# Attention scores on the two halves of the TensorE array: three 64-row matmuls per component in place of two 128-row ones

## The chip, the cores and the metric

The kernel runs on one core of a Trainium2 chip. The metric is the device time of one execution in microseconds, and the figure quoted is the median of several runs. Inputs, outputs and intermediate tiles are float32; large matmuls read float32 data through TensorE's fp32r form.

## What is computed

One layer of a hybrid encoder over 2048 positions of width 1024: a normalised input is projected, four heads of differential attention and four heads of a gated linear recurrence (HGRN2) work side by side on the projection, an output projection and a residual follow, and then a gated feed-forward block with a short convolution. The part that matters here is the differential attention. Each head has two components with 64 features, `q` and `k` are normalised, and the mask lets a query see all keys up to the end of its own chunk of 64:

```python
s = jnp.einsum('bqhcd,bkhcd->bhcqk', qb, k).astype(jnp.float32) * scale
p = jax.nn.softmax(jnp.where(mask, s, -jnp.inf), axis=-1)
a = p[:, :, 0] - lam * p[:, :, 1]
return jnp.einsum('bhqk,bkhe->bqhe', a.astype(v.dtype), v)
```

## The kernel before

The work has four stages: the mixer (projections, attention, recurrence), the output projection, the up projection with the convolution, and the down projection. The change is in the mixer.

The mixer runs four times over the sequence, once for each head `s` (lines 256 to 514). A pass goes over eight blocks of 256 positions, two query tiles of 128 each, so there are 16 query tiles in a pass and 64 in all. For a block, `get_h` fetches the normalised and transposed input as a high and a low part, `proj_a`, `proj_b` and `proj_c` project it with `mm3` (lines 252 to 254, three fp32r matmuls for each eighth of the depth), `trans_qk` transposes q and k, `attn` makes scores and exponentials, `attn_o` combines the two components, transposes the result and multiplies by v, and `hgrn` and `hgrn_o` do the recurrence.

float32 accuracy out of fp32r matmuls comes from splitting an operand into a high part and the remainder. For the scores, `proj_a` writes each normalised 64-feature vector twice, side by side (`qn` with a factor 2, one GpSimd instruction at line 290). `trans_qk` then has four transposes (line 300), and after them 128 rows hold the same 64 features twice. ScalarE writes the high parts (lines 302 and 304). VectorE writes the low part of q (line 305), and in k it overwrites the lower 64 rows with the low part (line 307). A 128-row matmul with the doubled high part of q against this k gives q_high times (k_high + k_low) in one go, and a second one with the low part of q adds the rest:

```python
PE.matmul(sc[:, c0:c0 + cwd], lhsT=qT[:, 0, c, :], rhs=kt[:, c, 0:cwd], start=True, stop=False)
PE.matmul(sc[:, c0:c0 + cwd], lhsT=qT[:, 1, c, :], rhs=kt[:, c, 0:cwd], start=False, stop=True)
```

`attn` handles a query tile in segments of up to 1024 keys (`SEG`), one component after the other. A step of segment and component fills the PSUM tile `sc` (two banks, and only one buffer, `SCB` = 1), sets the masked corner (line 360), takes the maximum on VectorE (line 362), and takes the exponential with its sum on ScalarE (line 373, which is an ACTIVATE and an ACTIVATION_READ_ACCUMULATOR). With a second segment the running maximum (line 365), a correction factor (line 367) and the corrected sum (line 377) are kept. `attn_o` rescales the first segment (line 396), adds the weighted second component (line 400), transposes (line 406), copies (line 408) and multiplies with v (line 411).

The strings `ORDER`, `O0` and `OF` (lines 874 to 876) set in which order the steps of the blocks are written down. The framework's planner then orders the instructions of each engine from data dependencies, free buffers and this order, so that in the trace the matmuls of the score steps stand among those of projections, recurrence and value products. The program on the chip is this fixed order; an engine waits at an instruction whose inputs are late, with all behind it.

Of the kernel before, what the change touches and what calls it, by code (L numbers as in the profile page):

```python
# [18 lines left out]
P = 128  # L19
# [15 lines left out]
NU = S // BLK  # L35
# [27 lines left out]
def hymba_kernel(ctx, tc, x, ln1_w, w_in, q_norm_w, k_norm_w, lam_q1, lam_k1, lam_q2, lam_k2,  # L63
# [25 lines left out]
    ident = cst.tile([P, P], F32, name="ident")  # L89
# [24 lines left out]
    neglam = few.tile([P, 1], F32, name="neglam")  # L114
# [70 lines left out]
    with ExitStack() as ms:  # L185
# [70 lines left out]
        for s in range(4):  # L256
# [16 lines left out]
            def proj_a(b, j):  # L273
                hT = HT_[b]
                kb = b // 2
                if b % 2 == 0 and j == 0:
                    kst[kb] = kv.tile([P, 2, 512], F32R, name="kst", tag="kst")
# [8 lines left out]
                ACT.activation(out=qn[:, :, 0, :], in_=qr, func=AF.Square)  # L286
                ss = sm.small([P, 4], F32, name="ssq", tag="ssq", bufs=2)
                DVE.tensor_reduce(out=ss, in_=qn[:, :, 0, :], axis=AX.X, op=ALU.add)
                r = rstd(sm, ss, 4, 64, "rq")
                POOL.tensor_tensor(  # L290
                    out=qn, in0=qr.rearrange("p g (o e) -> p g o e", o=1).broadcast_to([P, 4, 2, 64]),
                    in1=r.rearrange("p (g o e) -> p g o e", o=1, e=1).broadcast_to([P, 4, 2, 64]), op=ALU.mult)
                QN[b, j] = qn

            def trans_qk(b, j):
                qn = QN.pop((b, j))
                ko = ((2 * b + j) % 4) * P
                tp = pa.tile([P, 4, P], F32, name="tpq", tag="pj", bufs=PJB)
                for g in range(4):
                    PE.transpose(tp[:, g, :], qn[:, g].rearrange("p a e -> p (a e)"), ident)  # L300
                qT = wk.tile([P, 2, 2, P], F32R, name="qT", tag="qT", bufs=QTB)
                ACT.activation(out=qT[:, 0], in_=tp[:, 0:2], func=AF.Copy, scale=qkw[:, 0:1])
                kd = kst[b // 2][:, :, ko:ko + P]
                ACT.activation(out=kd, in_=tp[:, 2:4], func=AF.Copy, scale=qkw[:, 1:2])
                DVE.scalar_tensor_tensor(out=qT[:, 1], in0=tp[:, 0:2], scalar=qkw[:, 0:1],
                                         in1=qT[:, 0].bitcast(F32), op0=ALU.mult, op1=ALU.subtract)
                DVE.scalar_tensor_tensor(out=kd[64:], in0=tp[64:, 2:4], scalar=qkw[64:, 1:2],
                                         in1=kd[64:].bitcast(F32), op0=ALU.mult, op1=ALU.subtract)
                QS[b, j] = qT

            def proj_b(b, j):
# [27 lines left out]
            def attn(b, j):  # L339
                i = 2 * b + j  # L340
                n = (i + 1) * P
                segs = [(k0, min(n, k0 + SEG)) for k0 in range(0, n, SEG)]
                two = len(segs) > 1
                qT = QS.pop((b, j))
                pt = {}
                nms = {}
                ls = {}
                ws = [None, None]
                for si, (k0, k1) in enumerate(segs):
                    for c in range(2):  # L350
                        w = k1 - k0
                        sc = ps.tile([P, SEG], F32, name="sc", tag="sc", bufs=SCB)
                        last = si == len(segs) - 1
                        for c0 in range(0, w, 512):
                            cwd = min(512, w - c0)
                            kt = kst[(k0 + c0) // 512]
                            PE.matmul(sc[:, c0:c0 + cwd], lhsT=qT[:, 0, c, :], rhs=kt[:, c, 0:cwd], start=True, stop=False)  # L357
                            PE.matmul(sc[:, c0:c0 + cwd], lhsT=qT[:, 1, c, :], rhs=kt[:, c, 0:cwd], start=False, stop=True)  # L358
                        if last:
                            DVE.memset(sc[0:64, w - 64:w], -3.0e38)  # L360
                        nm = sm.small([P, 1], F32, name="nm", tag="nm", bufs=8)
                        DVE.tensor_reduce(out=nm, in_=sc[:, 0:w], axis=AX.X, op=ALU.max, negate=True)  # L362
                        if si > 0:
                            nm2 = sm.small([P, 1], F32, name="nm2", tag="nm", bufs=8)
                            DVE.tensor_tensor(out=nm2, in0=nm, in1=nms[c], op=ALU.min)
                            wv = sm.small([P, 1], F32, name="wv", tag="wv", bufs=8)
                            ACT.activation(out=wv, in_=nms[c], func=AF.Exp, scale=-1.0, bias=nm2)
                            ws[c] = wv
                            nm = nm2
                        nms[c] = nm  # L370
                        p = pb.tile([P, SEG], F32, name="p", tag="p")
                        l = sm.small([P, 1], F32, name="l", tag="l", bufs=16)
                        ACT.activation(out=p[:, 0:w], in_=sc[:, 0:w], func=AF.Exp, bias=nm, accum_out=l)  # L373
                        pt[si, c] = p
                        if si > 0:
                            l2 = sm.small([P, 1], F32, name="l2", tag="l", bufs=16)
                            DVE.scalar_tensor_tensor(out=l2, in0=ls[c], scalar=ws[c], in1=l, op0=ALU.mult, op1=ALU.add)
                            l = l2
                        ls[c] = l
                AT[b, j] = (pt, ls, ws, segs, two, i)  # L380

            def attn_o(b, j):
                pt, ls, ws, segs, two, i = AT.pop((b, j))
                r1 = sm.small([P, 2], F32, name="r1", tag="r12")
                DVE.reciprocal(out=r1[:, 0:1], in_=ls[0])
                DVE.reciprocal(out=r1[:, 1:2], in_=ls[1])
                cc = sm.small([P, 2], F32, name="cc", tag="cc")
                DVE.scalar_tensor_tensor(out=cc[:, 0:1], in0=ls[0], scalar=r1[:, 1:2], in1=neglam, op0=ALU.mult, op1=ALU.mult)
                av = ps.tile([P, 512], F32, name="av", tag=AVT, bufs=AVB)
                if two:  # L390
                    DVE.tensor_tensor(out=cc[:, 1:2], in0=cc[:, 0:1], in1=ws[1], op=ALU.mult)
                for si, (k0, k1) in enumerate(segs):
                    w = k1 - k0
                    a = pt[si, 0]
                    if two and si == 0:
                        DVE.tensor_scalar(out=a[:, 0:w], in0=a[:, 0:w], scalar1=ws[0], scalar2=None, op0=ALU.mult)
                        c_ = cc[:, 1:2]
                    else:
                        c_ = cc[:, 0:1]
                    DVE.scalar_tensor_tensor(out=a[:, 0:w], in0=pt[si, 1][:, 0:w], scalar=c_, in1=a[:, 0:w],  # L400
                                             op0=ALU.mult, op1=ALU.add)
                    for c0 in range(0, w, 512):
                        nk = min(512, w - c0) // P
                        tp = ps.tile([P, 4, P], F32, name="tpa", tag="m", bufs=MB)
                        for kk in range(nk):
                            PE.transpose(tp[:, kk, :], a[:, c0 + kk * P:c0 + (kk + 1) * P], ident)
                        aT = wk.tile([P, 4, P], F32, name="aT", tag="aT", bufs=ATB)
                        ACT.copy(aT[:, 0:nk], tp[:, 0:nk])
                        for kk in range(nk):
                            kt = (k0 + c0) // P + kk  # L410
                            PE.matmul(av[:, 0:P], lhsT=aT[:, kk, :], rhs=vst[kt // 4][:, kt % 4, :],  # L411
                                      start=kt == 0, stop=kt == i)
# [466 lines left out]
SCB, PJB, MB = 1, 2, 2  # L879
# [33 lines left out]
```

## Time and profile before

| | |
|---|---|
| median of 3 runs | 2813.1 us (2809.25 to 2815.34) |
| the profiled execution, its own time | 2810.73 us |
| its span | 2809.0 us |
| busy share of the span | PE 96%, PE weight load 84%, DVE 70%, ACT 43%, POOL 39% |
| mean granted TensorE clock | 0.988 of full speed |
| end of the mixer's score steps | about 1253 us after the start of the span |

A matmul's recorded duration covers its way through the array, and the next one begins before it ends. The engine's price of a matmul is therefore the distance from its start to the next start, which a timeline shows, and not the mean duration in a group. PEld is the loading of the stationary operand, which goes beside the matmuls. A row of a group gives line, engine, operation, output and inputs, shape and count, then the busy time in us, the mean duration in ns, and the idle time of the engine just before with what ended it.

### The profile page before, as it was taken

Reading aid. Unit: us, or ns where it says so; the run is one execution under the profiler, and the core shown is the slowest. Engines: PE = TensorE matmul, PEld = TensorE weight load, DVE = VectorE, ACT = ScalarE, POOL = GpSimd, SP = SyncE. Lnnn points to the kernel's source line nnn. Section 1 sums busy time; section 2 is a strip of 40 time slices with the busy share of each in tenths; the row PEclk is TensorE's granted clock in tenths of the full one; section 3 lists DMA queues with packets and bytes.
Section 4 is the critical chain, followed back from the end, with each engine's and each line's share of the span. In section 5 each row is a group of like instructions: output and inputs, shape, how many; then the busy total and the mean of one; then the engine's idle time right before and its main releaser. Section 6 shows DMA issues by size and latency. Waiting matters only on the chain.

```text
span 2809.0 us, 42869 instructions
## 1 busy us (share of the span) xinstructions
PE 2687.4 (96%) x15298; PEld 2349.5 (84%) x15298; DVE 1967.7 (70%) x4049; ACT 1198.3 (43%) x2814; POOL 1090.6 (39%) x1137
## 2 busy tenths in 40 slices
PE   7999999999999999989999999999999998997988
PEld 7998999999999999978877888887888876786866
DVE  4677855676568656673338666678777779889898
ACT  4455533454345434453434444354433444333331
POOL 3232222222222222221244434434334347777775
PEclk9999999999999999999999999999999999999999
DMA  5222312131112221125753222234222224655665
GB/s 185 98 83 97 119 68 72 64 121 68 68 69 88 74 74 64 38 90 191 250 179 123 90 80 78 90 128 135 83 75 90 83 90 158 220 207 187 217 229 190
DMA packets 245557, 331.33 MB, mean 118 GB/s; under 512 B 16367, under 2 KB 203103, under 8 KB 241247
## 3 DMA queue, kind: packets, MB, share of 16 engines
q1 hardware_dynamic: 245342, 328.59, 34.8%
q8 instruction: 121, 1.98, 0.3%
q14 instruction: 94, 0.76, 0.1%
HBM read 223.67 MB, written 104.86 MB: 117 GB/s over the span
## 4 chain that ended last, share of the span: by engine, by line
PE 70%; DVE 15%; POOL 5%; ACT 4%; issue 4%; DMA 2%; SPq 0%; DVEq 0%; POOLq 0%; ACTq 0%
PE q L680 9%; PE q L679 9%; PE q L678 9%; PE pj L252 4%; PE pj L254 4%; PE pj L253 4%; DVE SG L612 4%; PE av L411 4%; PE lt L436 3%; DVE TW L612 2%; PE sc L357 2%; PE pjc L253 2%; PE pjc L252 2%; PE pjc L254 2%; PE pjo L594 2%
## 5 line engine op out<-in xcount | busy, mean ns | idle before, releaser
L800 PE MATMUL pd<-TW,SG 128*128 128x512 f32 x616 | 247.4, 402 | 36.8 <-DVE acc L806 15.1
L679 PE MATMUL q<-xT,WS 128*128 128x512 f32 x704 | 274.4, 390 | 2.4 <-DVE xT L612 2.4
L678 PE MATMUL q<-xT,WS 128*128 128x512 f32 x704 | 274.2, 390 | 0.5 <-ACT xT L611 0.5
L680 PE MATMUL q<-xT,WS 128*128 128x512 f32 x704 | 274.1, 389 | 0.3 <-DVE WS L612 0.3
L801 PE MATMUL pd<-TW,SG 128*128 128x512 f32 x616 | 246.2, 400 | 10.5 <-DVE TW L612 10.4
L802 PE MATMUL pd<-TW,SG 128*128 128x512 f32 x616 | 244.4, 398 | 1.8 <-DVE SG L612 1.8
L611 ACT CAST WS<-st 128x512 fp32r<-128x512 f32 x176 | 108.5, 618 | 244.1 <-PE q L680 230.2
L679 PE MATMUL q<-xB,WS 128*128 128x512 f32 x528 | 206.5, 391 | 2.3 <-DVE xB L612 2.3
L680 PE MATMUL q<-xB,WS 128*128 128x512 f32 x528 | 206.5, 392 | 0.9 <-DVE WS L612 0.9
L678 PE MATMUL q<-xB,WS 128*128 128x512 f32 x528 | 206.2, 391 | 1.1 <-ACT xB L611 1.0
L373 ACT ACTIVATE p<-sc,nm 128x1024 f32<-128x1024 f32 (+4 forms) x192 | 165.6, 862 | 96.9 <-DVE nm L362 96.0
L612 POOL TENSOR_TENSOR WS<-st,WS 128x512 fp32r<-128x512 f32 x44 | 87.2, 1982 | 279.4 <-ACT WS L611 272.5
L362 DVE TENSOR_REDUCE nm<-sc 128x1 f32<-128x1024 f32 (+4 forms) x192 | 174.2, 908 | 18.5 <-PE sc L358 16.2
L252 PE MATMUL pj<-WA,hT 128*128 128x384 f32 x512 | 176.6, 345 | 2.6 <-DVE hT L239 2.6
L800 PEld LDWEIGHTS pd<-TW,SG 128*128 128x128 f32 x616 | 118.8, 193 | 69.6 <-DVE acc L806 13.2
L254 PE MATMUL pj<-WA,hT 128*128 128x384 f32 x512 | 175.6, 343 | 0.0
L253 PE MATMUL pj<-WA,hT 128*128 128x384 f32 x512 | 175.5, 343 | 0.0
L679 PEld LDWEIGHTS q<-xT,WS 128*128 128x128 f32 x704 | 132.3, 188 | 30.6 <-DVE xT L612 3.1
L678 PEld LDWEIGHTS q<-xT,WS 128*128 128x128 f32 x704 | 132.4, 188 | 28.3 <-ACT xT L611 0.9
L680 PEld LDWEIGHTS q<-xT,WS 128*128 128x128 f32 x704 | 132.3, 188 | 28.2 <-DVE WS L612 0.7
L611 ACT CAST WS<-rawu 128x512 fp32r<-128x512 f32 x132 | 82.1, 623 | 161.3 <-PE q L680 160.8
L801 PEld LDWEIGHTS pd<-TW,SG 128*128 128x128 f32 x616 | 119.1, 193 | 37.8 <-DVE TW L612 13.3
(415 smaller groups left out, 8014.5 us busy)
## 6 DMA issues: line engine op xcount, KB each, us to landing
hT<-hTd SPq DMA_DIRECT2D x24, 2048.0 KB, 8.9
rawu<-in_w_up_dram SPq DMA_DIRECT2D x176, 256.0 KB, 3.0
od<-acc SPq DMA_DIRECT2D x48, 512.0 KB, 3.4
acc<-od SPq DMA_DIRECT2D x46, 512.0 KB, 4.4
gd<-c SPq DMA_DIRECT2D x176, 128.0 KB, 1.9
G<-gd SPq DMA_DIRECT2D x24, 768.0 KB, 4.7
xt<-in_x_dram SPq DMA_DIRECT2D x32, 512.0 KB, 4.1
hTd<-hT SPq DMA_DIRECT2D x8, 2048.0 KB, 7.9
```

What stands on the lines that cost most here:

```text
L252: PE.matmul(dst, lhsT=lh, rhs=rh, start=dt == 0, stop=False)
L253: PE.matmul(dst, lhsT=lh, rhs=rl, start=False, stop=False)
L254: PE.matmul(dst, lhsT=ll, rhs=rh, start=False, stop=dt == ND - 1)
L362: DVE.tensor_reduce(out=nm, in_=sc[:, 0:w], axis=AX.X, op=ALU.max, negate=True)
L611: ACT.copy(dst[:, 0], src)
L612: eng.tensor_tensor(out=dst[:, 1], in0=src, in1=dst[:, 0].bitcast(F32), op=ALU.subtract)
L678: PE.matmul(dst, lhsT=w[:, 0, cs], rhs=b_[:, 0, dt], start=dt == 0, stop=False)
L679: PE.matmul(dst, lhsT=w[:, 0, cs], rhs=b_[:, 1, dt], start=False, stop=False)
L680: PE.matmul(dst, lhsT=w[:, 1, cs], rhs=b_[:, 0, dt], start=False, stop=dt == 3)
L800: PE.matmul(pd, lhsT=Sx[n][:, 0, k], rhs=w[:, 0], start=k == 0, stop=False)
L801: PE.matmul(pd, lhsT=Sx[n][:, 0, k], rhs=w[:, 1], start=False, stop=False)
L802: PE.matmul(pd, lhsT=Sx[n][:, 1, k], rhs=w[:, 0], start=False, stop=k == len(qs) - 1)
```

## The change

Each 64-feature vector of q and k is written once; a transpose handles two components at a time, so `trans_qk` has two of them, and rows 0 to 63 hold the first component and rows 64 to 127 the second. q and k each get a high and a low part in full. The scores of a component are three matmuls with 64 rows (high by high, high by low, low by high), and the six of both components alternate between the upper and the lower rows. A segment has 512 keys, and the two banks of `sc` hold both components of it. One reduction takes both maxima; the exponentials are two instructions. A running maximum is kept for each segment, and all correction factors of a query tile are made at its end.

```diff
-TOP, FEW, SMALL, SMALL2 = 480, 192, 320, 192
+TOP, FEW, SMALL, SMALL2 = 480, 192, 256, 192
-SEG = 1024
+SEG = 512
...
-                qn = pp.tile([P, 4, 2, 64], F32, name="qn", tag="qn")
+                qn = pp.tile([P, 4, 64], F32, name="qn", tag="qn")
...
+                POOL.tensor_tensor(out=qn, in0=qr, in1=r.rearrange("p (g e) -> p g e", e=1).broadcast_to([P, 4, 64]),
+                                   op=ALU.mult)
...
-                tp = pa.tile([P, 4, P], F32, name="tpq", tag="pj", bufs=PJB)
-                for g in range(4):
-                    PE.transpose(tp[:, g, :], qn[:, g].rearrange("p a e -> p (a e)"), ident)
-                qT = wk.tile([P, 2, 2, P], F32R, name="qT", tag="qT", bufs=QTB)
+                tp = pa.tile([P, 2, P], F32, name="tpq", tag="pj", bufs=PJB)
+                for g in range(2):
+                    PE.transpose(tp[:, g, :], qn[:, 2 * g:2 * g + 2].rearrange("p a e -> p (a e)"), ident)
+                qT = wk.tile([P, 2, P], F32R, name="qT", tag="qT", bufs=QTB)
                 kd = kst[b // 2][:, :, ko:ko + P]
...
+                for g, d in enumerate((qT, kd)):
+                    ACT.activation(out=d[:, 0], in_=tp[:, g], func=AF.Copy, scale=qkw[:, g:g + 1])
+                    DVE.scalar_tensor_tensor(out=d[:, 1], in0=tp[:, g], scalar=qkw[:, g:g + 1],
+                                             in1=d[:, 0].bitcast(F32), op0=ALU.mult, op1=ALU.subtract)
...
+                for si in range(ns):
+                    w = min(SEG, n - si * SEG)
+                    kt = kst[si]
+                    sc = ps.tile([P, 2, SEG], F32, name="sc", tag="sc", bufs=SCB)
+                    for k, (x, y) in enumerate(((0, 0), (0, 1), (1, 0))):
+                        for c in range(2):
+                            cs = slice(64 * c, 64 * c + 64)
+                            PE.matmul(sc[:, c, 0:w], lhsT=qT[cs, x, :], rhs=kt[cs, y, 0:w], start=k == 0, stop=k == 2)
+                    if si == ns - 1:
+                        DVE.memset(sc[0:64, :, w - 64:w], -3.0e38)
+                    DVE.tensor_reduce(out=nm[:, si], in_=sc[:, :, 0:w], axis=AX.X, op=ALU.max, negate=True)
+                    if si:
+                        DVE.tensor_tensor(out=nm[:, si], in0=nm[:, si], in1=nm[:, si - 1], op=ALU.min)
+                    p = pb.tile([P, 2, SEG], F32, name="p", tag="p")
+                    for c in range(2):
+                        ACT.activation(out=p[:, c, 0:w], in_=sc[:, c, 0:w], func=AF.Exp, bias=nm[:, si, c:c + 1],
+                                       accum_out=l[:, c, si:si + 1])
+                    pt.append((p, w))
+                if ns > 1:
+                    fac = sm.small([P, 2, 4], F32, name="fac", tag="fac", bufs=4)
+                    for c in range(2):
+                        ACT.activation(out=fac[:, c, 0:ns], in_=nm[:, 0:ns, c], func=AF.Exp, scale=-1.0,
+                                       bias=nm[:, ns - 1, c:c + 1])
+                    DVE.tensor_tensor(out=l[:, :, 0:ns], in0=l[:, :, 0:ns], in1=fac[:, :, 0:ns], op=ALU.mult)
+                    ls = sm.small([P, 2], F32, name="ls", tag="ls", bufs=4)
+                    DVE.tensor_reduce(out=ls, in_=l[:, :, 0:ns], axis=AX.X, op=ALU.add)
...
+                for si, (p, w) in enumerate(pt):
+                    a = p[:, 0, 0:w]
+                    c_ = cc[:, 0:1]
+                    if si < ns - 1:
+                        DVE.tensor_scalar(out=a, in0=a, scalar1=fac[:, 0, si:si + 1], scalar2=None, op0=ALU.mult)
+                        c_ = cc[:, 1 + si:2 + si]
+                    DVE.scalar_tensor_tensor(out=a, in0=p[:, 1, 0:w], scalar=c_, in1=a, op0=ALU.mult, op1=ALU.add)
```

The transposes, copies and value products of `attn_o` stay one set for each 512 keys, as they were.

## Rows read from the trace of the kernel before

**Rows 1.** Busy time of each engine in stretches of the span. The first four rows are the mixer from its first score step on, the fifth is the mixer with its start, and the sixth is all that follows. Columns: stretch, its length, then busy us and instructions (x) of PE, PEld, DVE, ACT and POOL, the granted TensorE clock, the DMA share, GB/s.
```profile
45.00:350.00 305.00, 294.72 (x2141) 278.63 (x2139) 217.48 (x695) 162.52 (x452) 81.49 (x145) 0.98 0.29 102
350.00:650.00 300.00, 294.42 (x2167) 278.12 (x2166) 199.93 (x651) 136.40 (x398) 73.08 (x130) 1.00 0.22 76
650.00:950.00 300.00, 293.83 (x2160) 277.08 (x2159) 199.24 (x653) 135.36 (x396) 73.89 (x131) 1.00 0.23 78
950.00:1258.00 308.00, 291.65 (x2103) 272.96 (x2102) 202.69 (x649) 134.03 (x383) 77.50 (x124) 0.98 0.19 66
0.00:1258.00 1258.00, 1203.27 (x8735) 1133.48 (x8736) 840.48 (x2688) 589.75 (x1671) 322.87 (x572) 0.99 0.25 86
1258.00:2809.00 1551.00, 1484.11 (x6565) 1215.99 (x6563) 1127.22 (x1362) 608.53 (x1143) 767.72 (x565) 0.99 0.44 144
```

**Rows 2.** The page's chain of work that ended last, its shares of the span by engine.
```profile
PE 70%; DVE 15%; POOL 5%; ACT 4%; issue 4%; DMA 2%; SPq 0%; DVEq 0%; POOLq 0%; ACTq 0%
```

**Rows 3.** Waits of the mixer (0 to 1258 us): who waited for whom, us in total, times, the longest in us.
```profile
PEld sc L357 <- ACT p L373: 16.7, 39, 1.7
PEld lt L436 <- DVE kS L445: 13.2, 23, 3.6
PE sc L357 <- ACT p L373: 6.1, 6, 1.5
```

**Rows 4.** Groups of PE in the mixer, shapes kept apart: the score matmuls by their number of keys, and the transposes of q and k.
```profile
L357 PE MATMUL sc<-kst,qT 128*128 128x512 f32 x224 | 97.3, 435 | 6.7 <-ACT p L373 5.7
L300 PE MATMUL tpq<-ident,qn 128*128 128x128 f32 x256 | 39.4, 272 | 0.0
L357 PE MATMUL sc<-kst,qT 128*128 128x384 f32 x32 | 12.5, 389 | 0.5 <-ACT p L373 0.3
L357 PE MATMUL sc<-kst,qT 128*128 128x256 f32 x32 | 10.1, 316 | 0.0
L357 PE MATMUL sc<-kst,qT 128*128 128x128 f32 x32 | 8.6, 270 | 0.2
```

**Rows 5.** Timeline of PE around 567 us, matmuls with 256 columns one behind the other. Columns here and in the other timelines: start in us, duration in us, engine, line, operation, output and inputs, shape, count.
```profile
566.54 0.28 PE L252 MATMUL pjc<-hT,WC 128*128 128x256 f32 x1
...
567.26 0.28 PE L252 MATMUL pjc<-hT,WC 128*128 128x256 f32 x1
```

**Rows 6.** Timeline of PE around 577 us: matmuls with 384 columns, then the four of a score step with 1024 keys, then 384 columns again.
```profile
575.74 0.33 PE L254 MATMUL pj<-WA,hT 128*128 128x384 f32 x1
...
576.61 0.40 PE L357 MATMUL sc<-kst,qT 128*128 128x512 f32 x1
576.84 0.40 PE L358 MATMUL sc<-kst,qT 128*128 128x512 f32 x1
577.08 0.40 PE L357 MATMUL sc<-kst,qT 128*128 128x512 f32 x1
577.31 0.39 PE L358 MATMUL sc<-kst,qT 128*128 128x512 f32 x1
577.53 0.34 PE L253 MATMUL pj<-WA,hT 128*128 128x384 f32 x1
```

**Rows 7.** Timeline of PE from 570.5 us: value products (L411, full float32, each recorded as two matmuls), transposes (L406) and a state product (L472, full float32), then the rest of a score step.
```profile
570.54 1.99 PE L411 MATMUL av<-vst,aT 128*128 128x128 f32 x16
572.38 0.60 PE L406 MATMUL tpa<-ident,p 128*128 128x128 f32 x4
572.81 0.39 PE L472 MATMUL sp<-ig,kt__7572 128*128 128x128 f32 x2
572.95 0.48 PE L358 MATMUL sc<-kst,qT 128*128 128x512 f32 x1
573.27 0.39 PE L357 MATMUL sc<-kst,qT 128*128 128x512 f32 x1
573.50 0.40 PE L358 MATMUL sc<-kst,qT 128*128 128x512 f32 x1
```

**Rows 8.** Timeline of one score step with 1024 keys, from its first matmul to the first matmul of the next step; other work of the engines is left out.
```profile
589.42 0.40 PE L357 MATMUL sc<-kst,qT 128*128 128x512 f32 x1
...
591.19 1.22 DVE L362 TENSOR_REDUCE nm<-sc 128x1 f32<-128x1024 f32 x1
592.44 1.12 ACT L373 ACTIVATE p<-sc,nm 128x1024 f32<-128x1024 f32 x1 [0.38 <-DVE nm L362]
593.45 0.19 ACT L373 ACTIVATION_READ_ACCUMULATOR p<-sc,nm 128x1 f32 x1
...
593.70 0.50 PE L357 MATMUL sc<-kst,qT 128*128 128x512 f32 x1
```

**Rows 9.** Groups of ACT, DVE and POOL in the mixer: the exponentials of all sizes, those of 512 keys, the reading of their sums, the rescaling of a first segment, and the doubled normalisation of q and k.
```profile
L373 ACT ACTIVATE p<-sc,nm 128x1024 f32<-128x1024 f32 (+4 forms) x192 | 165.6, 862 | 96.9 <-DVE nm L362 96.0
L373 ACT ACTIVATE p<-sc,nm 128x512 f32<-128x512 f32 x16 | 10.9, 680 | 7.6 <-DVE nm L362 7.5
L373 ACT ACTIVATION_READ_ACCUMULATOR p<-sc,nm 128x1 f32 x192 | 37.4, 195 | 0.0
L396 DVE TENSOR_SCALAR p<-p,wv 128x1024 f32<-128x1024 f32 x32 | 24.0, 749 | 4.9 <-ACT wv L367 4.7
L290 POOL TENSOR_TENSOR qn<-qr,rq_r 128x512 f32<-128x512 f32 x64 | 69.7, 1090 | 5.0
```

More of the change, by code (lines that the diff above doesn't have):

```diff
@@ L276, in proj_a @@
                 if b % 2 == 0 and j == 0:
-                    kst[kb] = kv.tile([P, 2, 512], F32R, name="kst", tag="kst")
+                    kst[kb] = kv.tile([P, 2, SEG], F32R, name="kst", tag="kst")
                     vst[kb] = kv.tile([P, 4, P], F32, name="vst", tag="vst")
@@ L284, in proj_a @@
                 ACT.copy(vst[kb][:, i % 4, :], pj[:, 256:384])
-                qn = pp.tile([P, 4, 2, 64], F32, name="qn", tag="qn")
-                ACT.activation(out=qn[:, :, 0, :], in_=qr, func=AF.Square)
+                qn = pp.tile([P, 4, 64], F32, name="qn", tag="qn")
+                ACT.activation(out=qn, in_=qr, func=AF.Square)
                 ss = sm.small([P, 4], F32, name="ssq", tag="ssq", bufs=2)
-                DVE.tensor_reduce(out=ss, in_=qn[:, :, 0, :], axis=AX.X, op=ALU.add)
+                DVE.tensor_reduce(out=ss, in_=qn, axis=AX.X, op=ALU.add)
                 r = rstd(sm, ss, 4, 64, "rq")
-                POOL.tensor_tensor(
-                    out=qn, in0=qr.rearrange("p g (o e) -> p g o e", o=1).broadcast_to([P, 4, 2, 64]),
-                    in1=r.rearrange("p (g o e) -> p g o e", o=1, e=1).broadcast_to([P, 4, 2, 64]), op=ALU.mult)
+                POOL.tensor_tensor(out=qn, in0=qr, in1=r.rearrange("p (g e) -> p g e", e=1).broadcast_to([P, 4, 64]),
+                                   op=ALU.mult)
                 QN[b, j] = qn
@@ L341, in attn @@
                 n = (i + 1) * P
-                segs = [(k0, min(n, k0 + SEG)) for k0 in range(0, n, SEG)]
-                two = len(segs) > 1
+                ns = (n + SEG - 1) // SEG
                 qT = QS.pop((b, j))
[L345 to L349, printed above, removed]
-                    for c in range(2):
[L351 to L379, printed above, removed]
@@ L380, in attn @@
-                AT[b, j] = (pt, ls, ws, segs, two, i)
+                pt = []
+                nm = sm.small([P, 4, 2], F32, name="nm", tag="nm", bufs=4)
+                l = sm.small([P, 2, 4], F32, name="l", tag="l", bufs=6)
+                fac = None
+                for si in range(ns):
[12 more added lines that the diff above has]
+                    p = pb.tile([P, 2, SEG], F32, name="p", tag="p")
+                    for c in range(2):
+                        ACT.activation(out=p[:, c, 0:w], in_=sc[:, c, 0:w], func=AF.Exp, bias=nm[:, si, c:c + 1],
+                                       accum_out=l[:, c, si:si + 1])
+                    pt.append((p, w))
@@ L382, in attn_o @@
+                AT[b, j] = (pt, ls, fac, i)
             def attn_o(b, j):
-                pt, ls, ws, segs, two, i = AT.pop((b, j))
+                pt, ls, fac, i = AT.pop((b, j))
                 r1 = sm.small([P, 2], F32, name="r1", tag="r12")
[L385 to L388, printed above, removed]
+                DVE.reciprocal(out=r1, in_=ls)
@@ L389, in attn_o @@
+                cc = sm.small([P, 4], F32, name="cc", tag="cc")
+                DVE.scalar_tensor_tensor(out=cc[:, 0:1], in0=ls[:, 0:1], scalar=r1[:, 1:2], in1=neglam, op0=ALU.mult, op1=ALU.mult)
                 av = ps.tile([P, 512], F32, name="av", tag=AVT, bufs=AVB)
[L390 to L412, printed above, removed]
@@ new lines, in attn_o @@
+                ns = len(pt)
+                if ns > 1:
+                    DVE.tensor_scalar(out=cc[:, 1:ns], in0=fac[:, 1, 0:ns - 1], scalar1=cc[:, 0:1], scalar2=None, op0=ALU.mult)
+                for si, (p, w) in enumerate(pt):
[5 more added lines that the diff above has]
+                    DVE.scalar_tensor_tensor(out=a, in0=p[:, 1, 0:w], scalar=c_, in1=a, op0=ALU.mult, op1=ALU.add)
+                    nk = w // P
+                    tp = ps.tile([P, 4, P], F32, name="tpa", tag="m", bufs=MB)
+                    for kk in range(nk):
+                        PE.transpose(tp[:, kk, :], a[:, kk * P:(kk + 1) * P], ident)
+                    aT = wk.tile([P, 4, P], F32, name="aT", tag="aT", bufs=ATB)
+                    ACT.copy(aT[:, 0:nk], tp[:, 0:nk])
+                    for kk in range(nk):
+                        kt = si * (SEG // P) + kk
+                        PE.matmul(av[:, 0:P], lhsT=aT[:, kk, :], rhs=vst[kt // 4][:, kt % 4, :],
+                                  start=kt == 0, stop=kt == i)
```

8 lines of the change are left out of this document (2 added, 6 removed).

## The prediction

> **What bounds the kernel now.** I read the stretches first. In the mixer from 45 to 1258 us PE is busy in 1174.6 of 1213 us, VectorE in two thirds of the time, ScalarE and GpSimd in less than half [rows 1]. The granted clock there is 0.98 to 1.00, the level of 2.4 GHz, so no clock is to be won back. The chain that ended last agrees: 70% of it is PE [rows 2]. The waits say what is left over: PE stands still before a score step, for the exponential of the step before to free the only score buffer, for 16.7 + 6.1 = 22.8 us in 45 of 192 cases, and this is the largest wait in its way there; the recurrence's for VectorE comes next with 13.2 us in the weight loads [rows 3]. So the mixer is paid in matmul issue time, and a part of it that vanishes or is added counts nearly in full. The change touches nothing behind 1258 us.
>
> The price of a matmul is the distance to the next start. Four score matmuls of 512 columns take 577.53 - 576.61 = 0.92 us, 0.23 each; the five of 384 columns before them 0.174 each [rows 6]; 256 columns take 0.72 / 6 = 0.12 [rows 5]. With 128 columns it is no longer the columns that count: four transposes take 0.43 us, 0.11 each, and sixteen value matmuls 1.84 us, 0.115 each [rows 7]. A quarter of the columns costs half of the time; I read 0.11 as the price of loading 128 columns of weights, below which no matmul with new weights comes.
>
> **The change part by part.**
>
> *Scores, how many.* A query tile i has i + 1 key tiles, four to a block of 512 keys. In a pass that makes 28 full blocks and 12 partial ones (four each of 128, 256 and 384 keys); in four passes 112 full ones and 16 of each partial width. The counts agree: 224 and 32 first matmuls, for two components [rows 4]. A block costs four matmuls now: 112 x 4 x 0.23 + 16 x 4 x (0.174 + 0.12 + 0.11) = 103.0 + 25.9 = 128.9 us. After the change it is six.
>
> *Scores, price of a 64-row matmul.* No row shows one, so it is bounded. Upper end: each takes its turn as the 128-row ones do, six for four, 128.9 x 1.5 = 193.4, which is +64.5 us. Lower end: the two halves run wholly side by side, weights too, three prices a block: 96.7, which is -32.2 us. I take halves that stream side by side, because upper and lower rows hold different weights, read different partitions and write different banks, while the weights are still loaded one after the other. A pair then costs the larger of 0.23 and two loads of 0.11. A full block is 3 x 0.23 = 0.69 us and a partial one 6 x 0.11 = 0.66: 77.3 + 31.7 = 109.0 us, or -19.9. The second half starts one load later than the first and the next 128-row matmul needs both, so I add 0.11 for each full block, +12.3. Scores: **-7.6 us**.
>
> The Trainium skill has a rule for this on the page "TensorE: Matmul & The Clock Gate", Part 3: matmuls on different row groups run concurrently, some 4 ns apart. By it alone the scores would come near the lower end, and the sum, as an estimate, to 2810.7 - 32.2 - 14.1 + 8 = 2772 us; no row here shows such a pair.
>
> *Change of the row form.* Going from 128 rows to 64 and back may cost something. The nearest row is a change of another kind, from full float32 to fp32r: two float32 matmuls and the first score matmul behind them take 573.27 - 572.81 = 0.46 us, just 2 x 0.115 + 0.23 [rows 7]. That change is free, and I take 0. The upper end is a pipeline that has to empty: a 512-column matmul is recorded with 0.40 us and followed after 0.23 [rows 6], so 0.17 us at each change.
>
> *Transposes.* 256 become 128 [rows 4], 128 x 0.11 = **-14.1 us**. No DMA and no place in an order string is changed.
>
> *The hold of the score buffer.* Today a step of 1024 keys holds it from 589.42 to 593.64 us: matmuls, maximum 1.22, exponential 1.12, reading of the sum 0.19, and the next matmul starts 0.06 later [rows 8]. Afterwards two exponentials of 512 come behind the maximum, 2 x (0.680 + 0.195) = 1.75 [rows 9] where 1.31 was, 0.44 longer. There are 160 steps for 192. If as many of them are late as now, 45 x 160 / 192 = 37.5, that is +16.5 us; if the planner covers them all, the 22.8 us vanish. Behind the waiting matmul stand projections and recurrence on PE, and for those wait VectorE and ScalarE. I take **+8**, half of the upper end, since the order is laid out with the longer hold known, and today covers three steps in four.
>
> *VectorE, ScalarE, GpSimd: nothing.* ScalarE has 320 exponentials of at most 0.680 + 0.195 for 165.6 + 37.4 us, at most +77 [rows 9], which takes it from 590 to 667 of 1258 us [rows 1]. VectorE rescales 96 pieces of 512 where it rescaled 32 of 1024: at most 96 x 0.749 - 24.0 = +48 [rows 9], on 840 of 1258. GpSimd's 69.7 us at line 290 shrink to about half. PE's work covers all three. If that cover were gone, the most is the 0.44 us of each of 160 steps, 70 us.
>
> *Sum.* -7.6 - 14.1 + 8 = -13.7 us. The profiled execution took 2810.73 us (span 2809.0), which gives 2797.0. It lies 2.4 us under the median of 2813.1; on the median the forecast is **2799 us**. Its own range is 2769 (all waits gone) to 2808 (full hold); 2756 if the second half's late start is gone as well.
>
> **The rivals.**
>
> *One after the other (slower).* PE takes the 64-row matmuls in turn, as the four of 512 columns in [rows 6] do, each 0.23 behind the other. The place is the score step on PE. 64.5 - 14.1 + 8 = +58.4 us, **2871 us**. The point of decision is the price of a pair in full blocks: the change breaks even where 336 pairs and 31.7 us of partial blocks cost 128.9 + 14.1 - 8, that is at 0.31 us with no late start. Side by side it is 0.23, in turn 0.46. For it: every row of before. Against it: all of those use all 128 rows.
>
> *Emptying at each change of form (slower).* Halves side by side, but every block of 512 keys pays twice for the change, 160 x 2 x 0.17 = 54.4 us: **2854 us**. It breaks even at 13.7 / 320 = 0.043 us a change. For it: the step in [rows 7] was cut in two by value products, so the planner may make more than 320 changes. Against it: the free change in [rows 7].
>
> The Trainium skill states this rival as a rule, on "TensorEngine Tiling (Array Packing)", Key Properties: switching the tiling mode, other than the tile, drains TensorE. The trace of before has no 64-row matmul by which to agree or differ.
>
> *Weights side by side too (faster still).* Scores -32.2, transposes -14.1, no hold: 2767 us; with the waits gone as well, 2744.
>
> *The change does not do what it says.* The planner may not keep the halves in turn, but put other matmuls between them. Then a half runs alone at 0.23 and the time drifts towards the first rival; its share is in that rival's chance.
>
> **How the numbers follow.** About 0.2%, 5.6 us, is what a measurement of this kernel can tell from no change. Chances: the forecast 0.42, one after the other 0.28, emptying 0.24, weights too 0.06. The forecast's case lies mostly under 2807.5 (0.38 of its 0.42). Emptying is faster only under about 0.025 us a change (0.02), same in 0.05, slower in 0.17. So faster 0.38 + 0.06 + 0.02 = 0.46, same 0.04 + 0.05 = 0.09, slower 0.28 + 0.17 = 0.45. Cases of both signs hold most of the chance: the likeliest alone has 2769 to 2808. The range goes from 2770 to 2871; above it lies half of the first rival, below it part of the last, together under 0.2.
>
> **What would show it.** In the profile after: two score matmuls with 64 rows whose starts are 0.11 us apart or less, and 0.23 to 0.25 from pair to pair (0.46 says one after the other); the first 128-row matmul behind a step coming 0.1 us later than its kind does elsewhere at most (0.17 or more says emptying); 128 transposes of q and k; waits of PE for the exponential between 0 and 40 us; the mixer's end near 1244 us, and the stages behind it as long as before. The prediction is wrong if a pair costs more than 0.31 us, if changes of form cost more than 0.04 us, or if the longer hold leaves PE idle for over 20 us more than now.

## The result and the profile after

The changed kernel is slower: 2847.9 us median of four runs (2846.5 to 2849.8) beside 2813.8 us for the kernel before on the same chip, a ratio of 1.0128 with a 95% interval of 1.0115 to 1.0140, or 34.1 us. The forecast was 2799 us. The direction was wrong; the time lies in the range given (2770 to 2871) and next to the rival "emptying at each change of form" (2854).

All of the loss is in the mixer, as far as a profile can place it. The last score step's sum is read at 1290.1 us where it was read at 1253.3; from there to the end it takes 1554.8 us where it took 1555.7. The stretches of the span, for comparison with [rows 1] (same columns: stretch, length, busy us and instructions of PE, PEld, DVE, ACT, POOL, granted clock, DMA share, GB/s):

```profile
45.00:350.00 305.00, 293.23 (x2141) 262.44 (x2142) 208.17 (x693) 163.43 (x508) 71.26 (x143) 0.99 0.28 100
350.00:650.00 300.00, 294.52 (x2157) 262.77 (x2157) 187.36 (x643) 137.41 (x455) 67.02 (x128) 1.00 0.22 76
...
0.00:1292.00 1292.00, 1233.13 (x8938) 1097.30 (x8938) 819.65 (x2735) 615.53 (x1966) 294.83 (x575) 0.99 0.24 84
1292.00:2845.00 1553.00, 1490.53 (x6552) 1220.84 (x6552) 1118.47 (x1362) 606.62 (x1137) 776.76 (x562) 0.98 0.43 144
```

PE is as full as before and at the same clock, 294.5 of 300 us in the second stretch in both kernels; the mixer just holds more PE time, 1233.1 us against 1203.3 in [rows 1]. Its idle time hardly grew: 1292.0 - 1233.1 = 58.9 us after, 1258.0 - 1203.3 = 54.7 before. So PE doesn't wait longer on balance; it takes longer for what it does.

The groups that answer to [rows 4] and [rows 9], of the mixer (busy us, mean ns, idle before):

```profile
L352 PE MATMUL sc<-kst,qT 64*128 64x512 f32 x672 | 127.2, 439 | 1.3 <-ACT p L360 1.1
L299 PE MATMUL tpq<-ident,qn 128*128 128x128 f32 x128 | 26.5, 282 | 0.0
L360 ACT ACTIVATE p<-sc,nm 128x512 f32<-128x512 f32 x224 | 152.4, 687 | 91.2 <-DVE nm L355 46.1 <-DVE nm L357 44.6
L360 ACT ACTIVATION_READ_ACCUMULATOR p<-sc,nm 128x1 f32 x320 | 63.9, 200 | 0.0
L389 DVE TENSOR_SCALAR p<-p,fac 128x512 f32<-128x512 f32 x96 | 45.7, 479 | 27.9 <-ACT fac L366 27.9
L290 POOL TENSOR_TENSOR qn<-qr,rq_r 128x256 f32<-128x256 f32 x64 | 41.0, 641 | 5.0
```

The counts are those of the forecast: 672 = 6 x 112 score matmuls of 512 keys, 128 transposes, 96 rescalings, 320 exponentials' sums.

What a score step costs now is in the timeline of PE (start, duration), one full step between projections of 384 columns:

```profile
589.17 0.33 PE L253 MATMUL pj<-WA,hT 128*128 128x384 f32 x1
589.35 0.34 PE L254 MATMUL pj<-WA,hT 128*128 128x384 f32 x1
589.61 0.96 PE L352 MATMUL sc<-kst,qT 64*128 64x512 f32 x6
590.51 0.44 PE L252 MATMUL pj<-WA,hT 128*128 128x384 f32 x1
590.79 0.34 PE L253 MATMUL pj<-WA,hT 128*128 128x384 f32 x1
590.97 0.33 PE L254 MATMUL pj<-WA,hT 128*128 128x384 f32 x1
```

and the weight loads of the same stretch:

```profile
589.17 0.19 PEld L254 LDWEIGHTS pj<-WA,hT 128*128 128x128 f32 x1
589.61 0.53 PEld L352 LDWEIGHTS sc<-kst,qT 64*128 64x128 f32 x6 [0.25 <-issue]
590.51 0.19 PEld L252 LDWEIGHTS pj<-WA,hT 128*128 128x128 f32 x1 [0.36 <-issue]
590.62 0.19 PEld L253 LDWEIGHTS pj<-WA,hT 128*128 128x128 f32 x1
590.79 0.19 PEld L254 LDWEIGHTS pj<-WA,hT 128*128 128x128 f32 x1
```

Four places are late. The projection at 589.35 is followed after 0.26 us, where projections of this width follow each other after 0.174 [rows 6]: +0.09. Inside the six, the pairs are 0.34 and then 0.23 us apart (medians over 89 uncut steps: 0.337 and 0.233): +0.10 in the first. From the last pair to the projection it is 0.33 in place of 0.23: +0.09. And from that projection to the next 590.79 - 590.51 = 0.28 in place of 0.174: +0.10. The loads say why. In ordinary work the next weights are loaded one matmul ahead, under the running one (the load at 590.62 for the matmul at 590.79). At 589.61 and at 590.51 the load begins together with its own matmul, after 0.25 and 0.36 us in which the weight path waited for nothing that the profile shows ("issue"). I read it as a load that waits until the array is empty; and since it had no head start, its own matmul and the one behind it come late. That is 0.38 us for a run of 64-row matmuls, **0.19 us for each change of form**. Behind some neighbours it is less: where a transpose of q and k follows (20 of the 89 steps), the fourth place is 0.06 and the run 0.33.

The waits that answer to [rows 3] (who for whom, us, times, longest), with those that are new:

```profile
PEld pj L252 <- issue: 10.7, 29, 2.8
PEld sc L352 <- ACT p L360: 8.8, 27, 1.5
PEld sc L352 <- issue: 8.6, 39, 0.4
PEld tpa L395 <- issue: 7.0, 13, 1.6
PEld lt L425 <- issue: 5.8, 18, 0.4
PE sc L352 <- ACT p L360: 2.4, 6, 1.3
```

The wait for the exponential fell from 22.8 us to 8.8 + 2.4 = 11.2. The "issue" waits ahead of score, projection, transpose and recurrence weights are new or larger, and they stand where the form changes. Of the chain that ended last PE now has 62% and VectorE 16%, beside 70% and 15% [rows 2].

### The profile page after: what moved, and what is told of

Read it like the earlier page. It is cut to its first block, busy times and chain, and to the rows that moved or that the text cites. A ratio compares the mean times of both kernels' runs of the same rounds, so it can differ in the third digit from the quotient of the medians.

```text
span 2844.9 us, 43603 instructions
## 1 busy us (share of the span) xinstructions
PE 2723.7 (96%) x15490; PEld 2318.1 (81%) x15490; DVE 1938.1 (68%) x4097; ACT 1222.2 (43%) x3102; POOL 1071.6 (38%) x1137
## 4 chain that ended last, share of the span: by engine, by line
PE 62%; DVE 16%; POOL 4%; ACT 4%; issue 3%; DMA 3%; DVEq 0%; SPq 0%; POOLq 0%; ACTq 0%
PE q L669 9%; PE q L668 9%; PE q L667 9%; DVE SG L601 4%; PE pj L252 3%; PE pj L254 3%; PE av L400 3%; PE pj L253 3%; PE sc L352 3%; PE lt L425 3%; DVE TW L601 2%; PE pjo L583 2%; PE pjo L585 2%; PE pjo L584 2%; DVE acc L795 2%
## 5 line engine op out<-in xcount | busy, mean ns | idle before, releaser
L360 ACT ACTIVATE p<-sc,nm 128x512 f32<-128x512 f32 (+3 forms) x320 | 197.2, 623 | 145.0 <-DVE nm L357 93.2
L601 POOL TENSOR_TENSOR WS<-st,WS 128x512 fp32r<-128x512 f32 x44 | 93.5, 2126 | 280.6 <-ACT WS L600 280.6
L355 DVE TENSOR_REDUCE nm<-sc 128x2 f32<-128x1024 f32 (+3 forms) x160 | 169.3, 1058 | 36.0 <-PE sc L352 34.7
L789 PEld LDWEIGHTS pd<-TW,SG 128*128 128x128 f32 x616 | 119.8, 195 | 68.3 <-DVE acc L795 12.7
L352 PE MATMUL sc<-kst,qT 64*128 64x512 f32 (+2 forms) x960 | 161.2, 406 | 2.5 <-ACT p L360 2.4
L252 PE MATMUL pj<-WB,hT 128*128 128x256 f32 x512 | 149.5, 292 | 3.2 <-ACT ig L313 2.7
```

What stands on the lines that cost most here:

```text
L252: PE.matmul(dst, lhsT=lh, rhs=rh, start=dt == 0, stop=False)
L352: PE.matmul(sc[:, c, 0:w], lhsT=qT[cs, x, :], rhs=kt[cs, y, 0:w], start=k == 0, stop=k == 2)
L360: ACT.activation(out=p[:, c, 0:w], in_=sc[:, c, 0:w], func=AF.Exp, bias=nm[:, si, c:c + 1], accum_out=l[:, c, si:si + 1])
L601: eng.tensor_tensor(out=dst[:, 1], in0=src, in1=dst[:, 0].bitcast(F32), op=ALU.subtract)
L789: PE.matmul(pd, lhsT=Sx[n][:, 0, k], rhs=w[:, 0], start=k == 0, stop=False)
```

## The experiments

Times are medians; "above" is the distance to the kernel before in the same set on the same chip (2812.1, 2811.8 and 2811.0 us in the three sets). By that measure the change is 34.1 us above.

**The new steps alone** (e1_full_rows). The steps of 512 keys and both components, the one reduction, the split exponentials and the late factors stay; q and k are doubled and transposed as before, and a component takes two matmuls with 128 rows.

```diff
...
-                    for k, (x, y) in enumerate(((0, 0), (0, 1), (1, 0))):
-                        for c in range(2):
-                            cs = slice(64 * c, 64 * c + 64)
-                            PE.matmul(sc[:, c, 0:w], lhsT=qT[cs, x, :], rhs=kt[cs, y, 0:w], start=k == 0, stop=k == 2)
+                    for c in range(2):
+                        for x in range(2):
+                            PE.matmul(sc[:, c, 0:w], lhsT=qT[:, x, c, :], rhs=kt[:, c, 0:w], start=x == 0, stop=x == 1)
```

> The changed kernel with the old row form put back: q and k doubled, four transposes, two 128-row matmuls a component; segments of 512 keys, one maximum and two exponentials a step stay as changed. Theory A (every change between 128-row and 64-row matmuls costs TensorE about 0.2 us, some 430 of them, and this alone made the kernel slower): the loss goes, and what is left is the shorter waiting for the score buffer, 2800 to 2815 us. Theory B (the new steps, their longer hold of the buffer and the new order of the instructions made it slower): it stays near 2848 us.

Measured: 2825.4 us, ratio 1.0049 (1.0034 to 1.0064), 13.3 us above, between the two figures expected. So the new steps cost 13 us by themselves, and the 64-row form 34.1 - 13.3 = 20.8 us more, although it has fewer transposes and cheaper scores. In this kernel the mixer's PE and the waits for the exponential stand so:

```profile
0.00:1271.00 1271.00, 1205.61 (x8750) 1132.58 (x8750) 853.36 (x2738) 628.91 (x1966) 324.47 (x575) 0.99 0.25 85
```

```profile
PEld sc L354 <- ACT p L362: 18.1, 38, 1.5
PE sc L354 <- ACT p L362: 9.2, 15, 1.3
```

PE is busy as long as before (1205.6 beside 1203.3) and idle 65.4 us, 10.7 more: here the loss is waiting, and in the 64-row kernel it is PE's own time. The waits for the exponential are 18.1 + 9.2 = 27.3 us here and 22.8 in [rows 3], so by them the longer hold of the score buffer is some 4.5 of the 13 us. The two kernels lose for different reasons.

**Six matmuls not cut** (e6_uncut). The planner puts other matmuls between the six of some steps: the order on the chip has 216 runs of 64-row matmuls for 160 steps, so 432 changes where the forecast's rival counted 320. A critical section around the six was to bring them back to 320.

```diff
+                    with tc.tile_critical():
+                        for k, (x, y) in enumerate(((0, 0), (0, 1), (1, 0))):
...
```

> The changed kernel, with the six matmuls of a step held together in the order of TensorE, so that there are 160 runs of 64-row matmuls and not 216: 112 changes of form fewer. Theory A: 112 x 0.2 = 22 us less, 2826 us. Theory B: no change that can be told, 2843 to 2853 us.

Measured: 3231.4 us, ratio 1.149 (1.1471 to 1.1509). The section makes the engines wait, 297.9 us in 160 waits of the score weights alone (the profile puts them down to "issue"). That swamps the question; nothing on the changes follows from it.

**More cuts** (e4_cut, e4_edge). A matmul of 128 rows and 64 columns with zero weights, which adds nothing to the scores, stands between the second and the third pair, so that each step is cut; in the control it stands ahead of the six, at the edge of a run.

```diff
                     for k, (x, y) in enumerate(((0, 0), (0, 1), (1, 0))):
                         for c in range(2):
                             ...
+                        if k == 1:
+                            PE.matmul(sc[:, 0, 0:64], lhsT=zero, rhs=kt[:, 0, 0:64], start=False, stop=False)
```

> The changed kernel with one 128-row matmul of 64 columns and zero weights put between the second and the third pair of each step: 160 matmuls and 320 changes of form more. Theory A: 64 us above the kernel with the same matmul ahead of the six, some 2930 us. Theory B: the same as that kernel, some 2866 us.

> The changed kernel with the same 128-row matmul of 64 columns and zero weights, ahead of the six, where the form changes anyway: 160 matmuls more, no change of form more. Both theories: 160 loads of weights of 0.11 us, 18 us more, 2866 us. It is the measure for the kernel that puts it in the middle.

Measured: cut 2897.0 us, ratio 1.0302 (1.0286 to 1.0317), with 732 changes; edge 2861.7 us, ratio 1.0175 (1.0160 to 1.0190), with 404. The difference is 35.2 us for 328 changes, 0.107 us each. The sign is clear, the size about half of what I had expected. In the timeline a cut is dear:

```profile
584.70 0.73 PE L355 MATMUL sc<-kst,qT 64*128 64x512 f32 x4
585.36 0.30 PE L357 MATMUL sc<-kst,zero 128*128 128x64 f32 x1
585.59 0.51 PE L355 MATMUL sc<-kst,qT 64*128 64x512 f32 x2
586.02 0.60 PE L430 MATMUL lt<-qP,kS 128*112 128x64 f32 x4
```

The second pair starts at 585.04 (inside the first row); from there to the next work it takes 586.02 - 585.04 = 0.98 us, where an uncut step has 0.23 + 0.33 = 0.56. That is 0.42 us a cut at the place, the extra matmul included; the control has that matmul too, and 35.2 / 160 = 0.22 us a cut is left in the time. Part of what PE loses at a change comes out of its waits, as the table at the end of this section shows.

**First in line** (e6b_first, e1_first). Raised priority keeps the six together without a section, with 330 changes; the control has the same priority and 128-row matmuls.

```diff
+                    with tc.high_priority():
+                        for k, (x, y) in enumerate(((0, 0), (0, 1), (1, 0))):
...
```

> The changed kernel with the six matmuls of a step marked as first in line for the planner, so that a step is rarely cut: 330 changes of row form in the order of TensorE and not 432, the same instructions. Theory A (the changes of form are the loss; 0.2 us each in the trace, 0.11 to 0.15 net so far): 11 to 20 us less, 2828 to 2837 us. Theory B (the new steps are the loss, whatever the form): no change that can be told, 2843 to 2853 us.

> The control to it: the changed kernel with the old 128-row form (2825 us), its score matmuls marked as first in line in the same way. Theory A: there is no form to change, so within 5 us of 2825. If being first in line helps by itself, it gains as much as the 64-row kernel does.

Measured: 2858.3 us, ratio 1.0168 (1.0153 to 1.0183), and 2841.0 us, ratio 1.0106 (1.0091 to 1.0121). To be first in line costs more than it saves, 15.9 us with 128 rows (29.2 above beside 13.3). Against its control the 64-row form costs 17.3 us with 330 changes, beside 20.8 us with 432. The difference of 3.5 us is inside the intervals (each ratio is uncertain by some 4 us), so the times of this pair neither confirm nor refute a price of each change. The gain that I had expected of fewer changes did not show in the time; PE's own time shows it (the table below).

**Two tiles for the two components** (e7_two_tiles). The new steps with 128-row matmuls again, but each component has its own PSUM tile of one bank, two buffers in all, with its own maximum.

```diff
...
-                    sc = ps.tile([P, 2, SEG], F32, name="sc", tag="sc", bufs=SCB)
+                    sc = [ps.tile([P, SEG], F32, name="sc", tag="sc", bufs=2) for c in range(2)]
...
```

> The changed kernel with the old 128-row form (2825 us, 13 us above the kernel before), and each component in a one-bank tile of its own, so that one bank comes free while the other is still read; two maxima and two running maxima a step. Theory B1 (the 13 us come from the one buffer, which is held until both exponentials are done): back to 2800 to 2815 us. Theory B2 (they come from the smaller and more numerous instructions of VectorE and ScalarE): 2825 to 2840 us.

Measured: 2832.3 us, ratio 1.0074 (1.0057 to 1.0091), 20.5 us above and 7 more than with the shared tile. If the hold of one score buffer were what the new steps cost, this was meant to give time back. But the waits for the exponential did not shrink, they grew from 27.3 to 27.1 + 13.2 = 40.3 us:

```profile
PEld sc L354 <- ACT p L363: 27.1, 50, 2.0
PE sc L354 <- ACT p L363: 13.2, 29, 1.8
```

VectorE has 320 reductions here where it had 160, so the run changed more than the hold and decides nothing about it. Against the hold as the main cause speak the waits of e1, 4.5 us above those of the kernel before.

**Not in turn** (e5_not_in_turn). All three matmuls of a component, then all three of the other.

```diff
-                    for k, (x, y) in enumerate(((0, 0), (0, 1), (1, 0))):
-                        for c in range(2):
-                            cs = slice(64 * c, 64 * c + 64)
+                    for c in range(2):
+                        cs = slice(64 * c, 64 * c + 64)
+                        for k, (x, y) in enumerate(((0, 0), (0, 1), (1, 0))):
```

> The changed kernel with the three matmuls of one component ahead of the three of the other, so that a half works alone but for one overlap in a step. If pairs gain what the trace shows (a pair of 512 columns for the price of one): two prices more a step, 112 x 0.46 + 16 x 2 x (0.174 + 0.12 + 0.11) = 64 us, 2912 us. If the six are bound by something else (weights, the changes of form alone): within 10 us of 2848.

Measured: 2850.9 us, ratio 1.0139 (1.0123 to 1.0154), no different from the change itself. In the order that the chip gets, 132 of the 160 steps stand uncut, with rows 0 to 63 three times and then rows 64 to 127 three times, and yet a step takes as long as in turn, 607.41 - 606.51 = 0.90 us:

```profile
606.51 0.97 PE L352 MATMUL sc<-kst,qT 64*128 64x512 f32 x6
607.41 0.65 PE L425 MATMUL lt<-qP,kS 128*126 128x64 f32 x4
```

In the records of another step the six begin at 597.139, 597.149, 597.476, 597.483, 597.707 and 597.714: three pairs. So do 113 of the 132 uncut steps, with at most 15 ns inside a pair. A time within 10 us of the change was to mean that something else than the pairs sets the pace; the records show that the pairs were there all the same.

**The change of form by itself** (e2_extra64, e3_extra128). The kernel before, steps and all, with one extra matmul of 64 columns ahead of each of its 192 score steps, with 64 rows or, as the control, with 128. Its result is overwritten by the step's first matmul.

```diff
+                        PE.matmul(sc[:, 0:64], lhsT=qT[0:64, 0, c, :], rhs=kst[k0 // 512][0:64, c, 0:64], start=True, stop=True)
```

> The kernel before, with one matmul of 64 rows and 64 columns ahead of each of its 192 score steps (its result is overwritten by the step's first matmul of start=True, so the scores stay the same). It brings 2 x 192 = 384 changes of form into a kernel whose score steps are otherwise untouched. Theory A (a change costs 0.11 to 0.2 us wherever it stands): 42 to 77 us above the same kernel with 128 rows in the extra matmul, so 2854 to 2905 us. Theory B (the changes cost nothing by themselves, the loss is in the shorter segments and the order that they bring): the same as that kernel within 5 us.

> The control of the run with 64 rows: the same 192 extra matmuls of 64 columns, with 128 rows, so without a change of form. Both theories: 192 x 0 to 0.11 us (a 128-column matmul with its own weights starts 0.11 us after the one before it), so 2812 to 2833 us.

Measured: 2869.6 us, ratio 1.0210 (1.0193 to 1.0227), and 2835.2 us, ratio 1.0088 (1.0073 to 1.0103); the control lies 2 us above its expected range. The 64-row matmul uses half of the rows and costs 34.4 us more; over 384 changes that is 0.09 us each. Nothing else differs: all other matmuls stand in the same order in the two traces. The theory that the changes are free falls; the price is under the 0.11 to 0.2 that I had put down. The two timelines, 64 rows first:

```profile
576.66 0.29 PE L252 MATMUL pjc<-hT,WC 128*128 128x256 f32 x1
576.79 0.28 PE L253 MATMUL pjc<-hT,WC 128*128 128x256 f32 x1
577.00 0.29 PE L354 MATMUL sc<-kst,qT 64*128 64x64 f32 x1
577.22 0.50 PE L358 MATMUL sc<-kst,qT 128*128 128x512 f32 x1
577.56 0.40 PE L359 MATMUL sc<-kst,qT 128*128 128x512 f32 x1
```

```profile
584.75 0.33 PE L253 MATMUL pj<-WA,hT 128*128 128x384 f32 x1
584.93 0.34 PE L254 MATMUL pj<-WA,hT 128*128 128x384 f32 x1
585.10 0.19 PE L354 MATMUL sc<-kst,qT 128*128 128x64 f32 x1
585.13 0.47 PE L358 MATMUL sc<-kst,qT 128*128 128x512 f32 x1
585.45 0.40 PE L359 MATMUL sc<-kst,qT 128*128 128x512 f32 x1
```

With 64 rows the extra matmul comes 0.21 us behind a projection of 256 columns (median of 76; 0.12 in the control, +0.09), and the score matmul 0.22 us behind it (mean of all 192; 0.09 in the control, +0.13). Behind that both have 0.32 to 0.34, so the late second matmul of a real run is there in either kernel; I read it as a matmul of 64 columns being too short to hide the next load. So this pair prices the emptying and hardly the load that it uncovers, which fits its finding less than the 0.19 us of a real run.

**PE's own time in the pairs.** Each page gives PE's busy time; the span less that is its idle time. A pair of kernels differs in them so (us):

| pair | changes of form more | PE busy | PE idle |
|---|---|---|---|
| e2_extra64, e3_extra128 | 384 | 2753.8 - 2709.8 = +44.0 | 114.1 - 123.3 = -9.2 |
| e4_cut, e4_edge | 328 | 2782.3 - 2732.5 = +49.8 | 111.3 - 124.8 = -13.5 |
| the change, e1_full_rows | 432 | 2723.7 - 2692.9 = +30.8 | 121.2 - 129.4 = -8.2 |
| e6b_first, e1_first | 330 | 2714.6 - 2703.5 = +11.1 | 141.4 - 136.4 = +5.0 |

In the first two pairs PE pays 0.11 and 0.15 us for a change, and a part of that is taken out of its waits. In the other two the cheaper scores (-32.2) and the missing transposes (-12.1, both worked out below) are in the sum; without them it is 75.1 us for 432 changes and 55.4 for 330, as an estimate 0.17 us each in both. With 102 changes fewer PE does save time; e6b_first loses it again in waits.

## Why the prediction was wrong

**The step that failed: "That change is free, and I take 0."** I priced the change of the row form at nothing from a change of another kind, float32 to fp32r [rows 7]. It costs 0.19 us at the place, 0.09 for the emptying and 0.10 for the next load that isn't hidden, a little more than the upper end of 0.17 that I had written down and passed over. The experiments that add changes find 0.09 and 0.107 us in the time, less than at the place. Of the two signs that I had written down for it, a price over 0.04 us shows it; a first 128-row matmul that is 0.17 us late does not, since that one is 0.09 late and the rest stands at three other places.

The trace of before held a nearer row, and I did not look for it. The last level of the recurrence (L436) has stationary operands of 64 columns, also a part of the array. Here is PE around two of its levels, 96 columns and then 64:

```profile
563.71 0.28 PE L254 MATMUL pjc<-hT,WC 128*128 128x256 f32 x1
563.83 0.47 PE L436 MATMUL lt<-qP,kS 128*96 128x64 f32 x4
564.12 0.36 PE L252 MATMUL pjc<-hT,WC 128*128 128x256 f32 x1
564.32 0.28 PE L253 MATMUL pjc<-hT,WC 128*128 128x256 f32 x1
...
565.83 0.45 PE L436 MATMUL lt<-qP,kS 128*64 128x64 f32 x4 [0.27 <-DVE kS L445]
566.20 0.39 PE L253 MATMUL pjc<-hT,WC 128*128 128x256 f32 x1
566.42 0.28 PE L254 MATMUL pjc<-hT,WC 128*128 128x256 f32 x1
```

and two of the loads:

```profile
564.09 0.19 PEld L252 LDWEIGHTS pjc<-hT,WC 128*128 128x128 f32 x1
...
566.20 0.19 PEld L253 LDWEIGHTS pjc<-hT,WC 128*128 128x128 f32 x1
```

Behind the level with 96 columns the projection starts at 564.12, 0.29 us after the level's first matmul, and its weights began to load before it. Behind the level with 64 it starts 0.37 us after, together with its load. On the way in, 28 of these levels stand behind a projection of 256 columns with a median distance of 0.21 us, where 0.12 is the rule. On the way out all 28 levels that stand before a projection of 256 columns take 0.37 us from start to start; the other levels in that place have a median of 0.325, but anything from 0.28 to 0.40, so only the way in gives a firm price. With its 0.09 in place of 0, and 320 changes, the forecast would have been -13.7 + 28.8 = +15 us, on the right side.

**Rival "emptying"**: right in mechanism. It had 320 changes of 0.17 us, 54.4 us; there are 432 of 0.19, 82 us. That it came near the measured time (2854) is in part luck: its changes were too few and too cheap, the pairs cheaper than it had them, a part of PE's loss came out of waits, and the new steps cost 13 us that it did not have. The Trainium skill states the rule on "TensorEngine Tiling (Array Packing)", Key Properties, and the traces agree with it: 0.25 and 0.36 us of "issue" ahead of the loads on the way in and out.

**Price of a pair**: better than forecast. I let the weights of a pair load one after the other (109.0 us, and 12.3 for a late second half); the two starts are 3 to 4 ns apart (median) and pairs of 512 columns 0.23, so the lower end holds for uncut steps: three prices a block, 96.7 us, -32.2 (a little less in all, since 28 of the 160 steps are cut). The Trainium skill's some 4 ns for matmuls on different row groups ("TensorE: Matmul & The Clock Gate", Part 3) agree with that. Rival "one after the other" falls, and e5 says that not even the order in the program brings it back.

**Transposes**: forecast -14.1, measured from start to start 29.8 to 19.0 us, -10.8.

**Hold of the score buffer**: wrong sign. I took +8; the waits for the exponential went from 22.8 to 11.2 us, -11.6. They grow to 27.3 us when the same steps are done without changes of form (e1). I read the fall as a PE that is slower elsewhere and lets the exponential catch up, a consequence of the loss and no gain.

**VectorE, ScalarE, GpSimd, "nothing"**: the second term put at nothing that failed. Their times moved within the bounds (rescaling 24.0 to 45.7 us, exponentials and sums 203.0 to 261.1, L290 69.7 to 41.0) and PE's work did cover most of them, but not all: e1 loses 13 us with PE's work unchanged, 10.7 of it as idle PE. It is spread over many of PE's waits for VectorE and ScalarE; the largest new one is 4.2 us, the transposes (L397) waiting for VectorE's weighted sum of the two components (L393). Which of the smaller instructions, the shared reduction, the factors at the end or the planner's new order is to blame was not separated, and stays open.

**The balance.** From the kernel before to e1 13.3 us, measured. From e1 to the change PE's busy time should move by the pairs, -32.2, the transposes, 31.1 to 19.0 = -12.1, and 216 runs x 0.38 = +82.1: +37.8 us. Measured are +30.8; with the other two terms as they are, a run costs 0.35 us on average. The waits for the exponential fall by 27.3 - 11.2 = 16.1 us, but others grow (the recurrence's state product for ScalarE, L461, from 4.8 to 11.0), so that PE's idle time falls by 8.2. Together that is 22.6 us between the two profiled executions, beside 20.8 between the medians.

The break-even follows. A full block gains 0.92 - 0.69 = 0.23 us and a run pays 0.38 between projections; a run of one block loses 0.15 and, as an estimate by the same numbers, a run of two blocks would win 0.08. The planner cuts the runs rather shorter (216 for 160 steps), and the PSUM tile holds one block of both components. A kernel with longer runs was not tried, and no version here beats the kernel before.

## What to carry to other kernels

Matmuls on the two halves of the array's rows did run side by side, but each switch between the full and the half form cost 0.11 to 0.19 us of TensorE, where a matmul of 512 columns costs 0.23: count the switches in the order that the chip gets, not the steps in the source, and make runs long enough to pay for two (an estimate here, not tried). Before a cost is set to zero for want of a row, search the trace for any instruction that already differs in the same way (fewer rows or fewer columns of weights) and read the distances to its neighbours. And test a change's parts one by one: here the smaller steps, which looked like bookkeeping, cost 13 of the 34 us. Read PE's busy and idle time beside the time: e6b_first saved busy time by fewer switches and lost it in waits, and the time alone showed nothing.

## What the runs showed of the hardware

- A matmul on the other half of the rows starts ahead of earlier ones in the program: three and three ran as three pairs, starts some 10 ns apart, 2850.9 us beside 2847.9 in turn (e5). On "TensorE: Matmul & The Clock Gate", Part 2, the Trainium skill says that the matmuls themselves stay in program order; these records say otherwise for two row groups, and the measurement decides.
- Weights for the two halves load side by side: pairs of 128 columns follow each other after as little as 0.11 us (the second and third pair of uncut steps of 128 keys), the price of one load of 128 columns in [rows 7], though each pair needs two.
- A form with 64 columns of weights pays on the way in like one with 64 rows: 0.21 us behind a projection of 256 columns in place of 0.12 (28 levels, the kernel before).
- A loss on TensorE need not reach the time in full: 49.8 us more busy time were 35.2 us in the time (e4), and 44.0 were 34.4 (e2).
